# Moving the second layer's gate blocks, a longer warm-up and a last output in three token parts

## The chip, the cores and the metric

The kernel runs on one core of a Trainium2 chip. The metric is the device time of one execution in microseconds (us); less is better. The core's engines are TensorE (PE for its matmuls, PEld for its weight loads), VectorE (DVE), ScalarE (ACT), GpSimd (POOL, unused here) and SyncE (SP), whose queue issues nearly all DMAs.

## The reference, cut to what matters

The program is one inference step of a two-layer backbone on 640 tokens (512 latent tokens and 128 context tokens) of width 1024. Each layer is one mixer:

```
shift, scale, gate = split(silu(cond) @ ada_w[l] + ada_b[l], 3)
h = rms_norm(x) * (1 + scale) + shift
u = h @ w_in[l]
y = concat(A differential attention, B gated 3-tap convolution,
           C latent attention, D neighbourhood attention), each times silu(its gate path)
x = x + gate * (y @ w_out[l])
```

Latent and context tokens have different `cond`. After the second layer there is a final RMSNorm, `y = x * rsqrt(mean(x*x) + eps) * g`. Keys and values of the context tokens are returned too.

## The kernel before, in words

**Precision.** Every large matmul works on split operands: a float32 value is held as a high part and a low part (both in the fp32r type), and a product is three matmuls: high x high, high x low, low x high. Each matmul instruction loads its own 128x128 stationary operand (a weight load on PEld) and then streams the moving operand, whose columns are tokens or output features. Plain float32 matmuls, as those with `ones` or `cs`, show as two matmul records each in the trace.

**Order of work.** The program first builds a list of operations (`Plan.add`), and a planner (`Plan.schedule`) then puts them in one order for each engine, by ready times from a table of costs (`price`, `transfer`) and by a priority: the place in the list plus the group's number in the table `SHIFT`. Each engine then runs its own list strictly in that order. All operations are issued from L464. In the planner's costs an fp32r matmul of n columns is `0.4375 * n + 6` ns, and the next matmul may follow 58 ns after.

**Front.** `keep_warm(WARM[0])` puts matmuls of `ones` by `ones` ahead of everything, so that TensorE has work before the first data arrive. Then the first 384 tokens of x (eight DMAs) and the first layer's eight shift-and-scale blocks are loaded, each block as two halves of 512 KB (`adaw`). `ada_rows` multiplies a half by `cs` in eight narrow matmuls, and after each of the first four halves it adds further `keep_warm` matmuls (`WARM[1]` to `WARM[4]`), which have the lowest priority but must all be run. `at(h)` places other loads among the halves: the pieces of the first projection's weights after the halves named in `WA`, the other tokens after those in `X1`. `rms_rows` adds the squares of x, sums them over the partitions by a matmul with `ones`, and takes the inverse root; `finish` makes `hh` and `hl` of one 128-row slice of h once that slice's block is there.

**Gate blocks and the second layer's blocks.** The first layer's four gate blocks and all twelve blocks of the second layer come later, one at each call of `ada_next`: two 512 KB loads into the `wraw` buffers (three buffers, shared with the weight pieces), eight narrow matmuls, a copy, and two small stores to a DRAM buffer `adram`. `ada_end` reads the stored rows back, reduces them, transposes them twice and adds the biases into `modA`, `modB` (shift and scale) and `modG` (gate). In the first layer there are eleven calls in the fills `d`, `qk0`, `qk1` and `b`, and eight in the output projection; so the last five of the 16 blocks fall into that projection, and the second layer's first projection waits for the end of the last `ada_end` (`gate[0]`).

**Fills.** The projections whose results aren't needed at once (`z`, `d`, `qk0`, `qk1`, `b`) are placed among the twelve attention heads by `FILL`; their matmuls take up what the softmax chains leave free on TensorE.

**Output projection.** For each part of `HALVES[l]` and each of eight output blocks `fb`, 24 matmuls (eight slices, three products) of a 128x128 stationary weight by `c1 - c0` tokens fill one bank; VectorE multiplies by the gate and adds x; ScalarE squares. After a part, `rms_rows` sums the squares, and in the last layer the result is scaled in two halves and stored. Before, both layers have two parts: tokens 0 to 384 and 384 to 640.

Of the kernel before, what the change touches and what calls it, by code (L numbers as in the profile page):

```python
# [13 lines left out]
F32 = mybir.dt.float32  # L14
# [6 lines left out]

L = 2
X1 = (4, 4, 4, 4, 4, 4, 4, 4)
WA = (2, 6, 11, 16)
LATE = (16, 17)
HALVES = (((0, 384), (384, 640)), ((0, 384), (384, 640)))
START = ((0, 384), (384, 640))
RMS = ((0, 8), (0, 8))
YK = (0, 1, 4, 5, 2, 6, 3, 7)
# [3 lines left out]
SWAP = 1290  # L33
SILU = 8
SLOW, LATER = 1.1, 800
WARM = (15, 10, 8, 4, 4)
SHIFT = {"": 38, "a0": 47, "a1": -28, "ada0": -8588, "av0": 6296, "av1": 3, "b0": 25951, "b1": 24557, "c0": -2462, "d0": 62, "d1": 33941, "f0.0": -174, "f0.1": 22, "f1.0": -183, "f1.1": 2841, "h0.0": -4317, "h0.1": 205, "h1.0": 7, "h1.1": -10499, "h10.0": 1418, "h10.1": -8, "h11.0": 638, "h11.1": 4686, "h2.0": -3351, "h2.1": -22079, "h3.0": -2855, "h4.0": -2974, "h4.1": -2909, "h5.0": -1, "h5.1": -9, "h6.0": 797, "h6.1": -6113, "h7.0": 20, "h7.1": 13278, "h8.0": 5300, "h9.0": -7596, "lam": 6901, "o0.0": -505, "o1.0": -80, "o1.1": 26, "p0.0": 162, "p0.1": -20, "p2.0": -2125, "p2.1": 432, "p3.0": -1337, "p3.1": 4371, "p4.0": -1388, "p4.1": -27369, "p7.0": -1727, "p7.1": 960, "p8.1": -18800, "pa0": 51, "pa1": -552, "qk00": -18970, "qk01": 10605, "qk10": 10903, "qk11": 14623, "x0": -3000, "x1": 6892, "x2": -1536, "y0": -1625, "y1": 9425, "y2": -77, "z0": -13, "z1": -227}
FILL = (('z', 4), ('d', 6), ('qk0', 7), ('qk1', 8), ('b', 12))
D = 1024
NT = 640  # L40
# [11 lines left out]
BIAS_W = 1792  # L52
# [430 lines left out]
def body(ctx: ExitStack, tc: tile.TileContext, i, o):  # L483
# [12 lines left out]
    R = Plan()  # L496
# [52 lines left out]
                R.ops[-1].prio += 10 ** 6  # L549
                R.ops[-1].cost = {"PE": 215}  # L550
    keep_warm(WARM[0])
    for op in R.ops[-WARM[0]:]:
        op.cost = {"PE": 320}

    modA = R.tile([128, L, 8, 2], F32, name="modA")
    modB = R.tile([128, L, 8, 2], F32, name="modB")
# [13 lines left out]
    def wpiece(l, name, idx):  # L570
        if l == 0 and name == "a":
            at(WA[idx])
            R.offset += WBOOST
        else:
            R.offset = 0
        off, kk, n = PIECES[name][idx]
        src = i["win"][l, off:off + 128 * kk * n].rearrange("(p c) -> p c", p=128)
        return wsplit(src, kk, n)

    def wsplit(src, kk, n, place=None):  # L580
        raw = R.tile([128, 1024], F32, name="wraw", tag="wraw", bufs=3)
# [13 lines left out]
    def at(h):  # L595

        R.offset = ada_at[min(h, 15)] + 7.5 * max(h - 15, 0) + 0.5 - len(R.ops)

    def ada_rows(l, blk, raws, warm):
        pa = (ttile if warm else mmtile)()  # L600
        for hf, raw in enumerate(raws):
            for k in range(4):
                PE.matmul(pa[32 * k:32 * k + 32, 0:256], cs[:, 4 * hf + k, :], raw[:, 256 * k:256 * k + 256],
                          start=(hf == 0), stop=(hf == 1))
            if warm and 2 * blk + hf < 4:
                keep_warm(WARM[1 + 2 * blk + hf], len(R.ops) - 1)
        sb = R.tile([128, 256], F32, name="adasb", bufs=1)
        S.activation(sb, pa[:, 0:256], AF.Copy)
        return sb

    def ada_first(l, blk, places):

        for hf in range(2):
            ada_at.append(len(R.ops))
            SP.dma_start(places[hf], i["adaw"][l, blk, hf])
        sb = ada_rows(l, blk, places, True)
        pb = ttile()
        for c in range(2):
            PE.matmul(pb[:, 2 * c:2 * c + 2], sb[:, 128 * c:128 * c + 128], sel, start=True, stop=True)
        R.need = len(R.ops) - 1  # L620
        V.tensor_scalar(modB[:, l, blk], pb[:, 0:2], sp[:, l, blk:blk + 1], None, op0=OP.add)
        V.tensor_scalar(modA[:, l, blk], pb[:, 2:4], b1[:, l, blk:blk + 1],
                        sp[:, l, 24 + blk:25 + blk], op0=OP.add, op1=OP.mult)

    def ada_block(l, blk):

# [11 lines left out]
    def ada_end(l, b0, b1_):  # L638
        group, R.group = R.group, f"ada{gate[1]}"
        nb = b1_ - b0  # L640
        m = 2 * nb
        tag, n = ("wraw", 1024) if l == 0 else ("bias", BIAS_W)
        rows = R.tile([128, n], F32, name=tag, tag=tag, bufs=3 if l == 0 else 1)[0:m, 0:1024]
        SP.dma_start(rows, adram[l, b0:b1_].rearrange("b s k c -> (b s) (k c)"))
        su = R.tile([128, 256], F32, name="adasb", bufs=1)[0:m]
        V.tensor_reduce(su, rows.rearrange("p (k c) -> p c k", k=4), AX.X, OP.add)
        pt = mmtile()
        for c in range(2):
            PE.transpose(pt[:, m * c:m * c + m], su[:, 128 * c:128 * c + 128], ident[0:m, 0:m])
        v = pt[:, 0:2 * m].rearrange("p (c b s) -> p b c s", c=2, b=nb)  # L650
        wide = lambda t, n: t[:, :, None].to_broadcast([128, n, 2])
        if nb == 12:
            V.tensor_add(modB[:, l], v[:, 0:8, 0], wide(sp[:, l, 0:8], 8))
            V.tensor_add(modA[:, l], v[:, 0:8, 1], wide(b1[:, l], 8))
            V.tensor_mul(modA[:, l], modA[:, l], wide(sp[:, l, 24:32], 8))
        for c in range(2):
            V.tensor_add(modG[:, l, c:8:2], v[:, nb - 4:nb, c], wide(sp[:, l, 16 + c:24:2], 4))
        R.group = group

    later = [(0, b) for b in range(8, 12)] + [(1, b) for b in range(12)]  # L660

    def ada_next(l):

        if l == 0 and later:
            ll, blk = later.pop(0)
            ada_block(ll, blk)
            if blk == 11:
                ada_end(ll, 8 if ll == 0 else 0, 12)
                gate[0] = len(R.ops) - 1

    def rms_rows(xv, cuts=(0, 8), wide=False):
        w = xv.shape[2]
# [163 lines left out]
    for l in range(L):  # L836
        if l == 0:
# [28 lines left out]
            for n, x in enumerate(x_cur):  # L866
                R.group = f"x{n}"
                first = len(R.ops)
                rstds.append(rms_rows(x, RMS[n], n == 0))
                for op in R.ops[first:]:  # L870
                    op.deps.add(table)
            for kt in range(8):
                for n, (x, c, rstd) in enumerate(zip(x_cur, START, rstds)):
                    R.group = f"{'xy'[n]}{min(kt, 2)}"
                    finish(0, x, kt, *c, rstd)
# [321 lines left out]
        def fill_d():  # L1197
            SP.dma_start(dvt[:, 5], i["cdv"][l])

            def ev_d(t, acc):  # L1200
                evac_copy(dvt[:, t], acc)
            R.need = dst.ops[0]
            ada_next(l)
            tm_seq(l, "dv", ev_d)
            R.need = None
            SP.dma_start(o["sdv"][l], dvt[:, 4])

        def fill_qk(p):
            if p:
                hl = R.tile([128, 2, 1408], F32R, name="hl")  # L1210
            else:
                hl = dst[:, 1536:].rearrange("p (a n) -> p a n", a=2)
            raw = R.tile([128, 128], F32, name="cd", bufs=2)
            SP.dma_start(raw, i["cdk"][l, p])
            R.ops[-1].deps.add(R.begun)
            split(hl[:, 0, NT + 256:NT + 384], hl[:, 1, NT + 256:NT + 384], raw, lambda t: t.bitcast(F32))
            R.need = len(R.ops) - 1
            wh, wl = wpiece(l, f"dq{p}", 0)

            def ev_q(hf, c, acc):  # L1220
                hi, lo = hl[:, 0, c], hl[:, 1, c]
                S.activation(hi, acc, AF.Copy, scale=0.125)
                V.scalar_tensor_tensor(lo, acc, 0.125, hi.bitcast(F32), op0=OP.mult, op1=OP.subtract)
            ada_next(l)
            fm_mm(wh, wl, ev_q)
            wh, wl = wpiece(l, f"dk{p}", 0)

            def ev_k(hf, c, acc):
                k = slice(NT + 384 * hf, NT + 256 + 512 * hf)
                split(hl[:, 0, k], hl[:, 1, k], acc, lambda t: t.bitcast(F32))  # L1230
                if hf:
                    st = R.tile([128, 128], F32, name="cd", bufs=2)
                    evac_copy(st, acc[:, 256:384])
                    SP.dma_start(o["sdk"][l, p], st)
            ada_next(l)
            fm_mm(wh, wl, ev_k, 256)
            R.need = None
            ready["qk", p] = hl
# [85 lines left out]
                    R.tile([128, 1024], F32R, name="wk", tag="ks", bufs=2)) for n in range(2)]  # L1324
        big2 = R.tile([128, 4, 1024], F32R, name="wyt", tag="yt")
        places += [(big2[:, 2 * n], big2[:, 2 * n + 1]) for n in range(2)]
        c0, c1 = HALVES[l][1]
        xall = R.tile([128, 2816], F32, name="xall", tag="hl")[:, :8 * (c1 - c0)].rearrange("p (k c) -> p k c", k=8)
        SP.dma_start(xall, xsrc[:, :, c0:c1].rearrange("k p c -> p k c"))
        for hf, (c0, c1) in enumerate(HALVES[l]):  # L1330
            R.group = f"o{hf}.{l}"
            xn = xns[hf]
            for fb in range(8):
# [3 lines left out]
                wh, wl = wo[fb]  # L1337
                w = c1 - c0
                if hf:
                    xo = xall[:, fb]  # L1340
                else:
                    xo = R.tile([128, NT], F32, name="xo", tag=("osb", "q3")[fb % 2], bufs=(2, 4)[fb % 2])
                    SP.dma_start(xo[:, :w], xsrc[fb, :, c0:c1])
# [11 lines left out]
                if l + 1 < L:  # L1355
                    SP.dma_start(xdram[fb, :, c0:c1], xn[:, fb])
            R.group = f"f{hf}.{l}"
            rstd = rms_rows(xn, (0, 7, 8) if l + 1 == L and hf == 1 else (0, 8))
            if l + 1 < L:
                for kt in range(8):  # L1360
                    finish(l + 1, xn, kt, c0, c1, rstd)
# [123 lines left out]
```

## Time and profile before

| what | us |
|---|---|
| time, median of 3 runs (825.54 to 825.94) | 825.73 |
| the profiled execution's own time | 825.87 |
| span of its trace, first to last instruction | 824.1 |
| TensorE busy with matmuls in the span | 799.7 |
| VectorE busy | 578.9 |
| ScalarE busy | 505.0 |

A view of the trace gives, for an instruction or a merged run of them, the start and the length in us from the span's start, the engine, the operation, what is written and read ("out<-in", with the shape as partitions x elements), and in brackets how long the engine sat idle before it and what it waited for. Matmuls are pipelined: the length of one is its latency, and what a matmul costs in a stream is the distance from one start to the next. In the view of stages the busy times stand in the order PE, PEld, DVE, ACT, POOL, each with its count of instructions, and then TensorE's granted clock as a share of 2.4 GHz, the DMA engines' busy share and GB/s.

### The profile page before, as it was taken

To read this page: it belongs to the slowest core of one execution; us is meant where nothing else is said; L and a number is where in the kernel's file an instruction comes from. 1 tells how busy PE (TensorE), PEld (TensorE's weight loads), DVE (VectorE), ACT (ScalarE), POOL (GpSimd) and SP (SyncE) were. 2 spreads that over 40 slices of the span, in tenths; PEclk is the share of its full clock that TensorE was granted. 3 is DMA by queue.
4 is the path that set the end of the run, shared out by engine and by line. 5 is a ranking of instruction groups with operands and counts; after the bars stand their busy time and mean duration, and the time that the engine had idled before them with its cause. 6 is when DMAs were issued, how large, how long until landed. Compare 5 with 4: busy or idle time off the path is not lost.

```text
span 824.1 us, 14974 instructions
## 1 busy us (share of the span) xinstructions
PE 799.7 (97%) x5570; PEld 746.0 (91%) x5570; DVE 578.9 (70%) x1296; ACT 505.0 (61%) x1108; POOL 0.2 (0%) x4
## 2 busy tenths in 40 slices
PE   7999999998999999999999999999999999999995
PEld 6789898998898888989998899999999989999995
DVE  3744499798674985837367636986987899876643
ACT  5852487677883874624237436866887878645432
POOL 0000000000000000000000000000000000000000
PEclk8999999999999999999999999999999999999998
DMA  9924533444562787756650355333146646823221
GB/s 313 364 100 109 169 88 83 114 133 119 173 162 83 186 259 203 254 170 215 238 193 30 89 139 165 105 79 104 61 108 159 145 106 184 254 70 90 84 77 52
DMA packets 50029, 120.15 MB, mean 146 GB/s; under 512 B 7940, under 2 KB 21892, under 8 KB 49956
## 3 DMA queue, kind: packets, MB, share of 16 engines
q1 hardware_dynamic: 49812, 119.11, 48.2%
q8 instruction: 44, 0.72, 0.4%
q14 instruction: 29, 0.24, 0.1%
q10 hardware_dynamic: 144, 0.07, 0.0%
HBM read 82.69 MB, written 6.59 MB: 108 GB/s over the span
## 4 chain that ended last, share of the span: by engine, by line
PE 85%; ACT 5%; DVE 4%; DMA 3%; issue 1%; SPq 1%; DVEq 0%; ACTq 0%
PE bank L464 81%; PE pair L464 5%; ACT t L464 2%; ACT thi L464 1%; DVE t L464 1%; DMA wraw<-adaw 1%; DMA bias<-bias 1%; DVE tlo L464 1%; DMA yt<-adaw 1%; SPq L464 1%; DVE mn L464 1%; DMA q<-hl 0%; DVE cst L464 0%; ACT avt L464 0%; DVE adasb L464 0%
## 5 line engine op out<-in xcount | busy, mean ns | idle before, releaser
L464 PE MATMUL bank<-hh,whi 128*128 128x320 f32 (+2 forms) x640 | 202.2, 317 | 0.3 <-ACT adasb L464 0.3
L464 PE MATMUL bank<-hh,wlo 128*128 128x320 f32 (+2 forms) x640 | 201.0, 315 | 0.0
L464 PE MATMUL bank<-hl,whi 128*128 128x320 f32 (+2 forms) x640 | 200.7, 314 | 0.0
L464 PEld LDWEIGHTS bank<-hh,whi 128*128 128x128 f32 x640 | 120.5, 188 | 2.8 <-issue 1.2
L464 PEld LDWEIGHTS bank<-hh,wlo 128*128 128x128 f32 x640 | 120.3, 188 | 2.4 <-issue 1.6
L464 PEld LDWEIGHTS bank<-hl,whi 128*128 128x128 f32 x640 | 120.6, 188 | 2.1 <-issue 1.2
L464 DVE TENSOR_TENSOR wlo<-wraw,whi 128x1024 fp32r<-128x1024 f32 (+1 forms) x64 | 76.5, 1195 | 62.8 <-ACT whi L464 62.5
L464 ACT ACTIVATE thi<-bank 128x512 fp32r<-128x512 f32 (+3 forms) x164 | 76.8, 486 | 49.1 <-PE bank L464 45.4
L464 PE MATMUL bank<-whi,hl 128*128 128x256 f32 (+2 forms) x320 | 105.9, 332 | 0.0
L464 PE MATMUL bank<-whi,hh 128*128 128x256 f32 (+2 forms) x320 | 105.1, 333 | 0.7 <-DVE adst L464 0.5
L464 PE MATMUL bank<-wlo,hh 128*128 128x256 f32 (+2 forms) x320 | 105.1, 329 | 0.0
L464 DVE TENSOR_TENSOR tlo<-bank,thi 128x512 fp32r<-128x512 f32 (+3 forms) x164 | 86.8, 548 | 16.9 <-ACT thi L464 16.1
L464 ACT ACTIVATE whi<-wraw 128x1024 fp32r<-128x1024 f32 (+1 forms) x64 | 66.3, 1035 | 51.9 <-PE bank L464 40.6
L464 DVE TENSOR_REDUCE mn<-pair 128x1 f32<-128x640 f32 x96 | 77.9, 816 | 7.0 <-PE pair L464 4.4
L464 ACT ACTIVATE t<-pair,mn 128x640 f32<-128x640 f32 x96 | 75.9, 792 | 9.2 <-DVE mn L464 6.1
L464 PE MATMUL bank<-par,t 128*128 128x128 f32 x456 | 79.6, 274 | 1.4 <-DVE tlo L464 1.4
L464 PE MATMUL pair<-ks,qs 96*128 96x320 f32 (+1 forms) x256 | 62.9, 327 | 4.6 <-ACT t L464 4.3
L464 PEld LDWEIGHTS bank<-whi,hh 128*128 128x128 f32 x320 | 60.1, 189 | 6.6 <-issue 0.8
L464 PE MATMUL bank<-thi,vs 128*128 128x256 f32 (+3 forms) x224 | 64.3, 295 | 0.8 <-ACT t L464 0.8
L464 PEld LDWEIGHTS bank<-whi,hl 128*128 128x128 f32 x320 | 60.3, 188 | 5.1 <-issue 1.6
L464 PEld LDWEIGHTS bank<-wlo,hh 128*128 128x128 f32 x320 | 60.4, 189 | 5.0 <-issue 1.2
L464 PE MATMUL bank<-tlo,vs 128*128 128x256 f32 (+3 forms) x224 | 64.0, 303 | 0.5 <-DVE tlo L464 0.5
(191 smaller groups left out, 1450.7 us busy)
## 6 DMA issues: line engine op xcount, KB each, us to landing
wraw<-win SPq DMA_DIRECT2D x52, 512.0 KB, 4.1
wraw<-adaw SPq DMA_DIRECT2D x32, 512.0 KB, 4.8
ks<-hl SPq DMA_DIRECT2D x48, 192.0 KB, 3.6
wraw<-wout SPq DMA_DIRECT2D x16, 512.0 KB, 3.9
bias<-bias SPq DMA_DIRECT2D x8, 896.0 KB, 6.8
ks<-hl SPq DMA_DIRECT2D x48, 96.0 KB, 2.2
qs<-hl SPq DMA_DIRECT2D x48, 80.0 KB, 2.1
qs<-hl SPq DMA_DIRECT2D x24, 160.0 KB, 2.5
```

Of the source, the lines that this page charges most:

```text
L464: done = getattr(engines[op.engine], method)(*[fix(x) for x in args], **{k: fix(x) for k, x in kw.items()})
```

## The change

- `HALVES[1]`: the second layer's output projection runs in three token parts, 0 to 384, 384 to 512 and 512 to 640, where it had two. The x rows of the last two parts are still loaded at once (`xall`).
- `later` is split by layer. The first layer's calls of `ada_next` now work off twelve blocks (its own four gate blocks and the second layer's eight shift-and-scale blocks); the second layer's four gate blocks come in the second layer's fill `b`, with an `ada_end` of their own. `ada_end` therefore runs three times, where it ran twice.
- `WARM` puts 34 matmuls ahead of the first data, where it had 15, and 4, 4, 4, 4 after the first four halves, where it had 10, 8, 4, 4.
- `WA` moves the four pieces of the first projection's weights one or two halves forward.
- Two dependencies are added in the front: the sum over x's first part is multiplied before the second half of block 0 (`second`), and the first weight piece is split only after that part's inverse root (`R.rooted`). The two operations that end a block (`modB`, `modA`) get a higher priority.
- `SHIFT` is a new table, so that the planner's order of all groups is another.

```diff
-WA = (2, 6, 11, 16)
+WA = (0, 5, 10, 15)
-HALVES = (((0, 384), (384, 640)), ((0, 384), (384, 640)))
+HALVES = (((0, 384), (384, 640)), ((0, 384), (384, 512), (512, 640)))
-WARM = (15, 10, 8, 4, 4)
+WARM = (34, 4, 4, 4, 4)
-SHIFT = {"": 38, "a0": 47, "a1": -28, "ada0": -8588, ...
+SHIFT = {"": 38, "a0": 44, "a1": 69, "ada0": -10519, "ada1": 1159, ...
...
     keep_warm(WARM[0])
-    for op in R.ops[-WARM[0]:]:
-        op.cost = {"PE": 320}
+    for n, op in enumerate(R.ops[-WARM[0]:]):
+        op.cost = {"PE": 340 if n < 14 else 215}
...
-        return wsplit(src, kk, n)
+        split_at = len(R.ops) + 1
+        w = wsplit(src, kk, n)
+        if l == 0 and name == "a" and idx == 0:
+            R.ops[split_at].deps.add(R.rooted)
+        return w
...
+            if warm and blk == 0:
+                second.append(len(R.ops))
...
+        for op in R.ops[-2:]:
+            op.prio -= 3000
...
-        tag, n = ("wraw", 1024) if l == 0 else ("bias", BIAS_W)
+        tag, n = ("wraw", 1024) if nb == 4 else ("bias", BIAS_W)
...
-        if nb == 12:
+        if nb == 8:
...
-        for c in range(2):
-            V.tensor_add(modG[:, l, c:8:2], v[:, nb - 4:nb, c], wide(sp[:, l, 16 + c:24:2], 4))
+        for c in range(2 if nb == 4 else 0):
+            V.tensor_add(modG[:, l, c:8:2], v[:, :, c], wide(sp[:, l, 16 + c:24:2], 4))
...
-    later = [(0, b) for b in range(8, 12)] + [(1, b) for b in range(12)]
+    later = ([(0, b) for b in range(8, 12)] + [(1, b) for b in range(8)], [(1, b) for b in range(8, 12)])
...
-        if l == 0 and later:
-            ll, blk = later.pop(0)
+        if later[l]:
+            ll, blk = later[l].pop(0)
+            gate[1] = l
             ada_block(ll, blk)
-            if blk == 11:
-                ada_end(ll, 8 if ll == 0 else 0, 12)
-                gate[0] = len(R.ops) - 1
+            if blk in (7, 11):
+                ada_end(ll, 0 if blk == 7 else 8, blk + 1)
+                if l == 0:
+                    gate[0] = len(R.ops) - 1
...
+                if n == 0:
+                    R.rooted = len(R.ops) - 1
                 for op in R.ops[first:]:
                     op.deps.add(table)
+                    if n == 0 and "PE" in op.calls:
+                        for k in range(4):
+                            R.ops[second[1] + k].deps.add(op.n)
...
-            ada_next(l)
+            if l == 0:
+                ada_next(l)
...
-        c0, c1 = HALVES[l][1]
+        c0, c1 = HALVES[l][1][0], NT
...
-                    xo = xall[:, fb]
+                    xo = xall[:, fb, c0 - HALVES[l][1][0]:c1 - HALVES[l][1][0]]
...
-            rstd = rms_rows(xn, (0, 7, 8) if l + 1 == L and hf == 1 else (0, 8))
+            rstd = rms_rows(xn, (0, 7, 8) if l + 1 == L and hf == 2 else (0, 8))
```

The guard `if l == 0` stands at the calls of `ada_next` in the fills `d`, `qk0` and `qk1`; those in `b` and in the output projection have none.

## Rows read from the trace of the kernel before

**Rows 1.** The page: busy time by engine.
```profile
PE 799.7 (97%) x5570; PEld 746.0 (91%) x5570; DVE 578.9 (70%) x1296; ACT 505.0 (61%) x1108; POOL 0.2 (0%) x4
```
**Rows 2.** Stages: stretch, its length, busy time by engine, granted clock, DMA.
```profile
10.70:14.00 3.30, 3.29 (x20) 2.19 (x24) 0.14 (x1) 0.00 (x0) 0.00 (x0) 0.50 1.03 420
...
62.00:320.00 258.00, 249.57 (x1798) 232.39 (x1797) 193.87 (x440) 175.46 (x400) 0.00 (x0) 1.00 0.50 141
320.00:427.00 107.00, 107.00 (x773) 98.14 (x772) 60.09 (x124) 43.66 (x85) 0.00 (x0) 1.00 0.69 224
427.00:680.00 253.00, 250.69 (x1716) 239.31 (x1716) 196.72 (x433) 174.07 (x388) 0.00 (x0) 1.00 0.39 107
680.00:814.00 134.00, 134.00 (x921) 132.12 (x920) 91.53 (x212) 70.98 (x150) 0.00 (x0) 1.00 0.39 117
```
**Rows 3.** Timeline of PE: first matmul of the last part, and what follows its last.
```profile
790.54 0.28 PE L464 MATMUL bank<-hh,whi 128*128 128x256 f32 x1
...
813.97 0.59 PE L464 MATMUL bank<-thi,ones 128*128 128x256 f32 x2
```
**Rows 4.** Timeline of PE and PEld: short runs of fp32r matmuls of 128 columns.
```profile
340.86 0.28 PE L464 MATMUL bank<-thi,vs 128*128 128x128 f32 x1
340.92 0.19 PEld L464 LDWEIGHTS bank<-tlo,vs 128*128 128x128 f32 x1
340.98 0.27 PE L464 MATMUL bank<-tlo,vs 128*128 128x128 f32 x1
341.03 0.19 PEld L464 LDWEIGHTS bank<-hh,wlo 128*128 128x128 f32 x1
341.09 0.36 PE L464 MATMUL bank<-hh,wlo 128*128 128x320 f32 x1
```
**Rows 5.** Timeline of PE: the same matmuls right behind one of 320 columns.
```profile
271.37 0.31 PE L464 MATMUL bank<-hh,wlo 128*128 128x320 f32 x1
271.51 0.33 PE L464 MATMUL bank<-ks,qs 128*128 128x128 f32 x2
271.68 0.28 PE L464 MATMUL bank<-k,q 128*128 128x128 f32 x1
271.79 0.36 PE L464 MATMUL bank<-hh,whi 128*128 128x320 f32 x1
```
**Rows 6.** Timeline behind the last projection matmul.
```profile
814.17 0.61 DVE L464 SCALAR_TENSOR_TENSOR cst<-bank,modG,hl 128x128 f32<-128x128 f32 x2 [1.29 <-PE bank L464]
...
815.28 0.70 PE L464 MATMUL bank<-tlo,ones 128*128 128x256 f32 x2 [0.72 <-ACT tlo L464]
816.02 0.47 ACT L464 ACTIVATE thi<-bank,epst 128x256 f32<-128x256 f32 x1 [0.25 <-PE bank L464]
...
816.97 2.36 DVE L464 TENSOR_TENSOR cst<-cst,thi 128x1024 f32<-128x1024 f32 x2 [2.19 <-ACT thi L464]
818.23 1.55 SPq L464 DMA_DIRECT2D yt<-cst  x2
```
**Rows 7.** Timeline of the front.
```profile
1.05 5.93 PE L464 MATMUL bank<-ones 128*128 128x128 f32 x30 [1.05 <-DVE ones L464]
...
10.71 1.08 PE L464 MATMUL bank<-yt,cs 128*32 128x256 f32 x8 [3.74 <-DMA yt<-adaw]
...
11.72 2.08 PE L464 MATMUL bank<-ones 128*128 128x128 f32 x8
...
18.97 1.36 PE L464 MATMUL bank<-ones 128*128 128x128 f32 x10
...
20.83 0.96 PE L464 MATMUL bank<-whi,hh 128*128 128x512 f32 x3
```
**Rows 8.** Groups of PE by form, from 8 to 31 us: the warm-up matmuls.
```profile
L464 PE MATMUL bank<-ones 128*128 128x128 f32 x46 | 7.7, 318 | 0.0
```
**Rows 9.** Waits of PE, from 280 to 330 us and from 425 to 450 us.
```profile
PE bank L464 <- DMA wraw<-adaw: 0.9, 1, 0.9
...
PE bank L464 <- DVE adasb L464: 0.5, 1, 0.5
```

More of the change, by code (lines that the diff above doesn't have):

```diff
@@ L35 @@
 SLOW, LATER = 1.1, 800
-WARM = (15, 10, 8, 4, 4)
-SHIFT = {"": 38, "a0": 47, "a1": -28, "ada0": -8588, "av0": 6296, "av1": 3, "b0": 25951, "b1": 24557, "c0": -2462, "d0": 62, "d1": 33941, "f0.0": -174, "f0.1": 22, "f1.0": -183, "f1.1": 2841, "h0.0": -4317, "h0.1": 205, "h1.0": 7, "h1.1": -10499, "h10.0": 1418, "h10.1": -8, "h11.0": 638, "h11.1": 4686, "h2.0": -3351, "h2.1": -22079, "h3.0": -2855, "h4.0": -2974, "h4.1": -2909, "h5.0": -1, "h5.1": -9, "h6.0": 797, "h6.1": -6113, "h7.0": 20, "h7.1": 13278, "h8.0": 5300, "h9.0": -7596, "lam": 6901, "o0.0": -505, "o1.0": -80, "o1.1": 26, "p0.0": 162, "p0.1": -20, "p2.0": -2125, "p2.1": 432, "p3.0": -1337, "p3.1": 4371, "p4.0": -1388, "p4.1": -27369, "p7.0": -1727, "p7.1": 960, "p8.1": -18800, "pa0": 51, "pa1": -552, "qk00": -18970, "qk01": 10605, "qk10": 10903, "qk11": 14623, "x0": -3000, "x1": 6892, "x2": -1536, "y0": -1625, "y1": 9425, "y2": -77, "z0": -13, "z1": -227}
+WARM = (34, 4, 4, 4, 4)
+SHIFT = {"": 38, "a0": 44, "a1": 69, "ada0": -10519, "ada1": 1159, "av0": 16007, "av1": 9, "b0": 20030, "b1": 26350, "c0": -2945, "c1": 42, "d0": -15, "d1": 38724, "f0.0": -2291, "f0.1": 28, "f1.0": -149, "f1.1": -6505, "f2.1": 5395, "h0.0": -10485, "h0.1": 156, "h1.0": 530, "h1.1": -10253, "h10.0": -8183, "h10.1": 5207, "h11.0": 1303, "h11.1": -4230, "h2.0": -7939, "h2.1": -11378, "h3.0": -4585, "h3.1": -5938, "h4.0": -1665, "h4.1": -3836, "h5.0": 361, "h5.1": 5772, "h6.0": -3668, "h6.1": -5092, "h7.0": -1594, "h7.1": 11755, "h8.0": 8691, "h8.1": -2253, "h9.0": -8898, "h9.1": 127, "lam": 9366, "o0.0": -433, "o0.1": -17292, "o1.0": 19, "o1.1": 37, "o2.1": 133, "p0.0": -4226, "p0.1": -2567, "p2.0": -4412, "p2.1": 431, "p3.0": 310, "p3.1": 4183, "p4.0": -365, "p4.1": 906, "p7.0": -1937, "p7.1": 8479, "p8.0": -7953, "p8.1": -163, "pa0": -333, "pa1": -9550, "qk00": -11029, "qk01": 7846, "qk10": 11602, "qk11": 14431, "x0": 2128, "x1": 639, "x2": -3103, "y0": -12028, "y2": -19596, "z0": -15, "z1": -227}
 FILL = (('z', 4), ('d', 6), ('qk0', 7), ('qk1', 8), ('b', 12))
@@ L597, in at @@
         R.offset = ada_at[min(h, 15)] + 7.5 * max(h - 15, 0) + 0.5 - len(R.ops)
+    second = []
     def ada_rows(l, blk, raws, warm):
@@ L641, in ada_end @@
         m = 2 * nb
-        tag, n = ("wraw", 1024) if l == 0 else ("bias", BIAS_W)
-        rows = R.tile([128, n], F32, name=tag, tag=tag, bufs=3 if l == 0 else 1)[0:m, 0:1024]
+        tag, n = ("wraw", 1024) if nb == 4 else ("bias", BIAS_W)
+        rows = R.tile([128, n], F32, name=tag, tag=tag, bufs=3 if nb == 4 else 1)[0:m, 0:1024]
         SP.dma_start(rows, adram[l, b0:b1_].rearrange("b s k c -> (b s) (k c)"))
@@ L1223, in ev_q @@
                 V.scalar_tensor_tensor(lo, acc, 0.125, hi.bitcast(F32), op0=OP.mult, op1=OP.subtract)
-            ada_next(l)
+            if l == 0:
+                ada_next(l)
             fm_mm(wh, wl, ev_q)
@@ L1234, in ev_k @@
                     SP.dma_start(o["sdk"][l, p], st)
-            ada_next(l)
+            if l == 0:
+                ada_next(l)
             fm_mm(wh, wl, ev_k, 256)
```

## The prediction

> **What bounds the kernel now.** I read the page first: TensorE is busy 799.7 us of 824.1, VectorE 578.9, ScalarE 505.0 [rows 1]. So the time is TensorE's own stream plus 24.4 us in which it stands still, and an edit counts if it changes that stream's length or one of those gaps. The view of stages says where the gaps are: 258.0 - 249.6 = 8.4 us between 62 and 320, none between 320 and 427, 2.3 between 427 and 680, none between 680 and 814 [rows 2]. That is 10.7 us in the middle, spread over many short waits. What is left lies at the ends: 3.74 us before the first block of weights [rows 7], and 10 us behind the last projection matmul [rows 3, 6].
>
> The busy share hides one more thing. A matmul's row gives its latency; its cost is the distance to the next start. I therefore read the timeline for starts, and for the shape that the change brings in: fp32r matmuls of 128 columns in a long stream. The kernel before has such matmuls only in runs of a few, among the attention heads of the context tokens.
>
> **The third part of the last output.** Before, the last part runs from 790.54 to 813.97 [rows 3]: 8 blocks of 24 matmuls are 192 of 256 columns, and the first part's sum of squares, one plain float32 matmul (0.6, an estimate from the 0.59 of the like pair at 813.97), runs among them; (23.4 - 0.6) / 192 = 0.119 us each. After, the same columns come as 2 x 192 = 384 matmuls of 128 columns, each again with its own weight load.
>
> What one of these costs has two bounds in the trace. Behind a matmul of 320 columns the first starts at 271.51, and the next, the second of the pair, 0.06 later (the pair is 0.33 long, one of them 0.27); then come 0.11 (271.68) and 0.11 (271.79) [rows 5]. In a run where the one before is also narrow the starts lie 0.12 and 0.11 apart (340.86, 340.98, 341.09), and the weight loads keep the same step (340.92, 341.03) [rows 4]. The reading: a wide matmul gives the next weight load time to finish under it, so that one narrow matmul gets through in its column time; a narrow one doesn't, and then the load, at 0.11, sets the pace. In the new parts every matmul stands behind a narrow one. I take 0.112, the nearest row being the run of narrow ones: 384 x 0.112 = 43.0 us against 192 x 0.119 = 22.8, so **+20.2**. Bounds: 0.058 gives 22.3 us (-0.5), 0.115 gives 44.2 (+21.4). Nothing hides this: TensorE has no gap between 680 and 814 [rows 2], and the planner's own cost (62 ns) is no row of the trace.
>
> Weighed against the skill: the Trainium skill, page "TensorE: Matmul & The Clock Gate", section "Weight-path perf modes", has a fast weight load for 128 weights of a type that isn't FP32, with no win for 4-byte types. Were fp32r loaded that way, the sum would be the one at 0.058; rows 4 speak against it.
>
> The new part has a sum of squares of its own: one more plain float32 matmul, two records, **+0.25** (0.12 each, from 1.36 us for ten [rows 7]). Its ScalarE and VectorE steps lie under 21 us of matmuls: below nothing and above nothing alike, unless VectorE, now a third idle there, were full.
>
> **The end.** Behind the last matmul stands a chain that works on 256 columns and will work on 128 [rows 6]: the two gate steps become one (0.61 to about 0.35, -0.26); three ScalarE steps of up to 0.47 lose at most half, I take 0.11 each (-0.33); the float32 pair goes from 0.70 to about 0.45 (-0.25); the two closing multiplies halve (2.36 to 1.2, -1.16); the last store carries half the bytes (0 to -0.7, I take -0.2). Together **-2.2**, between -1.6 and -2.9.
>
> **The front.** Before, 30 records of warm-up end at 6.98, TensorE idles 3.74 us, and the first block half, at 10.71, runs at a granted clock of 0.50 (1.2 GHz) [rows 2, 7]: the warm-up records are then 0.21 apart (2.08 for eight, one 0.58 long), later 0.12 [rows 7]. After: 68 records. The first 30 take until 6.98 as now, the other 38 take 38 x 0.12 = 4.6 at full clock and end near 11.5, or 38 x 0.21 = 8.0 and end near 15 at half clock. Busy without a break, the engine should keep the full clock, so 11.5: the first half starts some 0.8 late and is done in 0.6 in place of 1.1. What is late next is the rest of block 0, which now stands behind the sum over x.
>
> The possible gain: between 8 and 31 us the warm-up matmuls behind the halves take 7.7 us of TensorE's time [rows 8] and must be run in their place in the order, data or no data. After, they are 16 matmuls, 32 records, 3.8 us at 0.12. Half clock costs about 2 us of real work (four halves at 1.08 for 0.6 [rows 7]). The first projection starts at 20.83 [rows 7] and from then on its matmuls and the blocks' keep TensorE busy until 62, so an earlier start is kept. The ceiling is 3.9 + 2 - 0.8 = 5.1; the floor is a loss of 0.8, if the data, not TensorE, hold it up, because the weight pieces that `WA` moves forward push later halves back in SP's queue (512 KB each). I take **-3.5**, nearer to the ceiling, since TensorE ran without a gap there.
>
> **The gate blocks.** Four blocks (8 loads of 512 KB, 8 stores, 32 matmuls and their copies) leave the first layer's output projection, where TensorE has no gap, and come to the second layer's convolution, where it has next to none either: their matmuls cancel. The first layer's boundary waits 0.5 us for `ada_end`'s reduction [rows 9]; with fewer blocks that goes (**-0.5**). A third `ada_end` adds two transposes (about 0.3), a readback on SP and a reduction on VectorE: **+0.3**; its result is needed only in the output projection. The loads share three buffers with the weight pieces: such a load held TensorE up for 0.9 once in the first layer [rows 9], so 0 to +1; I take 0, DMA share being 0.39 in the new place and 0.69 in the old [rows 2].
>
> **The new order.** `SHIFT` changes the order of all groups. It can at best take away the 10.7 us of waits in the middle and may add as many. No row tells which; I take **0**, with 3 to either side.
>
> **Sum.** 20.2 + 0.25 - 2.2 - 3.5 - 0.5 + 0.3 = +14.55. On the profiled execution's 825.87 (span 824.1 and 1.8 around it) that is 840.4; the median, 825.73, is 0.14 lower, so **840.3**.
>
> **Rivals.**
> - *The loads are hidden after all* (6 in 100; the side of faster). Long streams let PEld run ahead, and each narrow matmul costs 0.058. The part then takes 22.3 us: 840.3 - 20.7 = 819.6. For it: the first narrow matmul behind a wide one. Against it: every later one. It decides if the spacing falls below about 0.074, where the narrow parts cost no more than the other gains return (0.112 - 14.5 / 384 = 0.074).
> - *Half hidden* (5 in 100): narrow matmuls alternate with waiting wide ones, or loads come in pairs, mean 0.085, 32.6 us, 829.9. The skill's page named above, section "Back-to-back issue gap", gives about 81 ns for a sustained stream of 128-column matmuls with their loads; by that rule the part takes 31.1 us and the sum is 828.4. No run of rows 4 is that fast.
> - *The longer warm-up does nothing* (16 in 100): data hold the front up, and it starts late instead: +0.8 for -3.5, 844.6, or with an order that costs some more, up to 847.
> - *The new order fills the middle* (5 in 100): half of the 10.7 us goes, 834.9.
> - The forecast as summed: 68 in 100, 837 to 843.
>
> **Chances and range.** Under 0.2% (1.7 us) a measurement of this kernel can't tell a change from none. Faster: the first rival, 0.06. Same: part of the second, 0.02. Slower: the rest, 0.92. The range 834 to 847 leaves out the two cases of hidden loads; it takes in both ends of the front, of the spacing (0.11 to 0.115, -0.8 to +1.2) and of the order.
>
> **What would show it.** In the trace after: the last part's 384 matmuls with starts and weight loads 0.11 apart, some 43 us from the end of the first part to the last sum of squares; about 8 us from there to the end; the granted clock at 1.00 from 10.7 on, and the first projection's start some 3 to 4 us before 20.83; as many gaps in the middle as before. The prediction is wrong if narrow starts lie under 0.08 apart, if the planner puts the narrow parts between wide ones, or if the middle's gaps move by more than 3 us.

## The result, and the profile after

The changed kernel takes 838.31 us (median of 4 runs, 838.17 to 841.85) against 825.63 for the kernel before in the same runs: ratio 1.0167, 95% interval 1.0138 to 1.0196. It is slower by 12.7 us; 840.3 was predicted, 834 to 847 the range. The profiled execution took 838.42, its span is 836.5.

The page's first part, busy time by engine:

```profile
PE 821.9 (98%) x5784; PEld 767.2 (92%) x5784; DVE 582.6 (70%) x1304; ACT 508.5 (61%) x1128; POOL 0.2 (0%) x4
```

TensorE is busy for 22.2 us more than in [rows 1], with 214 more matmuls: 192 from the third part, 38 from 19 more warm-up matmuls ahead, 20 fewer from the ten behind the halves, and four from a third sum of squares and a third `ada_end`. The stages, columns as in [rows 2]:

```profile
10.70:14.00 3.30, 3.30 (x29) 2.29 (x27) 0.25 (x1) 0.00 (x0) 0.00 (x0) 1.00 1.02 420
...
62.00:320.00 258.00, 252.63 (x1813) 234.99 (x1813) 190.15 (x432) 175.19 (x403) 0.00 (x0) 1.00 0.53 148
320.00:427.00 107.00, 106.99 (x750) 100.81 (x749) 73.12 (x156) 51.56 (x99) 0.00 (x0) 1.00 0.54 173
427.00:680.00 253.00, 251.67 (x1731) 239.20 (x1730) 191.14 (x424) 171.20 (x390) 0.00 (x0) 1.00 0.43 118
```

From 10.7 us on the granted clock is 1.00, where it was 0.50. TensorE's gaps between 62 and 680 are 5.4 + 1.3 = 6.7 us; they were 10.7. So two of the three places got better. The third is the end of TensorE's timeline, the first matmuls of the narrow parts and the last:

```profile
784.92 0.34 PE L464 MATMUL bank<-hh,yt 128*128 128x384 f32 x1
785.10 0.22 PE L464 MATMUL bank<-hh,whi 128*128 128x128 f32 x1
785.16 0.27 PE L464 MATMUL bank<-hl,whi 128*128 128x128 f32 x1
785.27 0.28 PE L464 MATMUL bank<-hh,wlo 128*128 128x128 f32 x1
785.38 0.28 PE L464 MATMUL bank<-hh,whi 128*128 128x128 f32 x1
785.49 0.28 PE L464 MATMUL bank<-hl,whi 128*128 128x128 f32 x1
...
828.68 0.27 PE L464 MATMUL bank<-hh,yt 128*128 128x128 f32 x1
828.79 0.43 PE L464 MATMUL bank<-thi,ones 128*128 128x128 f32 x2
```

Read the first column. The first narrow matmul, behind one of 384 columns, gives way after 0.06; from the second on they start 0.11 apart, to the end of the part. The two narrow parts and the sum between them run from 785.10 to 828.79, 43.7 us; the one part that they replace ran from 790.54 to 813.97, 23.4 us [rows 3]. The chain behind, which answers to [rows 6]:

```profile
829.00 0.35 DVE L464 SCALAR_TENSOR_TENSOR cst<-bank,modG,hl 128x128 f32<-128x128 f32 x1 [1.66 <-PE bank L464]
...
829.74 0.49 PE L464 MATMUL bank<-tlo,ones 128*128 128x128 f32 x2 [0.51 <-ACT tlo L464]
830.27 0.37 ACT L464 ACTIVATE thi<-bank,epst 128x128 f32<-128x128 f32 x1
...
831.01 1.29 DVE L464 TENSOR_TENSOR cst<-cst,thi 128x512 f32<-128x512 f32 x2 [1.66 <-ACT thi L464]
831.73 1.34 SPq L464 DMA_DIRECT2D yt<-cst  x2
```

And the front, TensorE alone, against [rows 7]:

```profile
1.04 10.79 PE L464 MATMUL bank<-ones 128*128 128x128 f32 x68 [1.04 <-DVE ones L464]
11.76 0.64 PE L464 MATMUL bank<-yt,cs 128*32 128x256 f32 x8
12.33 1.16 PE L464 MATMUL bank<-ones 128*128 128x128 f32 x8
...
17.62 1.38 PE L464 MATMUL bank<-ones 128*128 128x128 f32 x10
...
19.84 0.50 PE L464 MATMUL bank<-whi,hh 128*128 128x512 f32 x1
...
58.18 0.40 PE L464 MATMUL bank<-whi,hl 128*128 128x512 f32 x1
```

The last row is the last matmul of the first layer's first projection; before, it started at 61.65. Before, 26 warm-up records stood inside that projection, 18 of them in one run; after, four do:

```profile
23.01 2.17 PE L464 MATMUL bank<-ones 128*128 128x128 f32 x18
```

Cut at four points of TensorE's timeline, the two traces differ thus (us):

| stretch | before | after | difference |
|---|---|---|---|
| start to the last matmul of the first projection | 61.65 | 58.18 | -3.47 |
| from there to the first matmul of the last output | 695.37 | 693.38 | -1.99 |
| first part, 384 columns | 33.52 | 33.54 | 0.0 |
| remaining columns, to the last sum of squares | 23.43 | 43.69 | +20.26 |
| the end behind | 10.09 | 7.69 | -2.40 |
| span | 824.06 | 836.48 | +12.4 |

In the second row TensorE's idle time fell from 10.7 to 6.8 us. Without the idle time that stretch grew, from 684.6 to 686.6, so only half of what the gaps gave was won.

### The profile page after: what moved, and what is told of

It is laid out like the page before. It is cut to its first block, busy times and chain, and to the rows that moved or that the text cites. A ratio compares the mean times of both kernels' runs of the same rounds, so it can differ in the third digit from the quotient of the medians.

```text
span 836.5 us, 15439 instructions
## 1 busy us (share of the span) xinstructions
PE 821.9 (98%) x5784; PEld 767.2 (92%) x5784; DVE 582.6 (70%) x1304; ACT 508.5 (61%) x1128; POOL 0.2 (0%) x4
## 4 chain that ended last, share of the span: by engine, by line
PE 91%; DMA 3%; DVE 2%; ACT 2%; SPq 1%; issue 1%; DVEq 0%; ACTq 0%
PE bank L464 85%; PE pair L464 6%; DMA wraw<-adaw 1%; ACT t L464 1%; SPq L464 1%; DMA ks<-adst 1%; DMA wraw<-wuq 0%; DVE tlo L464 0%; ACT thi L464 0%; DMA wraw<-win 0%; DVE wlo L464 0%; ACT whi L464 0%; DVE mn L464 0%; DVE adasb L464 0%; DVE t L464 0%
## 5 line engine op out<-in xcount | busy, mean ns | idle before, releaser
L464 PE MATMUL bank<-hh,whi 128*128 128x320 f32 (+3 forms) x656 | 205.9, 315 | 0.6 <-ACT yt L464 0.5
L464 PE MATMUL bank<-hl,whi 128*128 128x320 f32 (+3 forms) x656 | 206.2, 315 | 0.0
L464 PE MATMUL bank<-hh,wlo 128*128 128x320 f32 (+3 forms) x656 | 205.1, 314 | 0.0
L464 PEld LDWEIGHTS bank<-hh,whi 128*128 128x128 f32 x656 | 123.6, 189 | 3.4 <-issue 1.2
L464 PEld LDWEIGHTS bank<-hl,whi 128*128 128x128 f32 x656 | 123.8, 189 | 2.5 <-issue 1.6
L464 PEld LDWEIGHTS bank<-hh,wlo 128*128 128x128 f32 x656 | 123.5, 189 | 2.3 <-issue 1.2
```

The lines of the kernel that those rows point to most:

```text
L464: done = getattr(engines[op.engine], method)(*[fix(x) for x in args], **{k: fix(x) for k, x in kw.items()})
```

## The experiments

The prediction's theory: the narrow matmuls each cost a weight load, and that is the whole loss. Its rival: the parts are neutral and the loss sits in the gate blocks or the new order.

**Two parts again.** In the changed kernel:

```diff
-HALVES = (((0, 384), (384, 640)), ((0, 384), (384, 512), (512, 640)))
+HALVES = (((0, 384), (384, 640)), ((0, 384), (384, 640)))
...
-            rstd = rms_rows(xn, (0, 7, 8) if l + 1 == L and hf == 2 else (0, 8))
+            rstd = rms_rows(xn, (0, 7, 8) if l + 1 == L and hf == 1 else (0, 8))
```

> The changed kernel with the second layer's output projection back in two token parts; all else as changed, and the order of every engine up to that projection is the same. Theory (the narrow parts cost their weight loads, +20.3 us, +0.25 for a third sum, and give back 2.4 at the end): 838.3 - 18.1 = 820.2 us, the last part 22.8 us of matmuls again, about 10 us behind it. Rival (the loss sits elsewhere, in the gate blocks or the new order, and the parts are neutral): 836 to 839.

Measured: 820.43 us (4 runs), ratio to the kernel before 0.9938, interval 0.9919 to 0.9957. The loss was the third part, and without it the rest of the change is a gain. This version beats both kernels. Its last part starts 0.12 apart again:

```profile
786.42 0.28 PE L464 MATMUL bank<-hh,whi 128*128 128x256 f32 x1
786.53 0.28 PE L464 MATMUL bank<-hl,whi 128*128 128x256 f32 x1
786.65 0.28 PE L464 MATMUL bank<-hh,wlo 128*128 128x256 f32 x1
```

> The two-part kernel a second time, on the same chip as the kernel with the front's changes alone. 820.4 us; ratio to the kernel before 0.994.

Measured: 819.07, ratio 0.9937, interval 0.9922 to 0.9951.

**The third part alone.** The kernel before with only `HALVES[1]`, `xall` and the last `rms_rows` of the change.

> The kernel before with nothing but the third token part; the order of every engine up to that projection is that of before. Theory: 825.6 + 18.1 = 843.7 us. Rival (parts neutral, loss elsewhere): 824 to 827.

Measured: 846.16, ratio 1.0246, interval 1.0227 to 1.0264; +20.8 us where 18.1 was expected. The 384 narrow matmuls start 0.113 apart on the mean, as expected. Behind them this kernel is slower than the changed one: from the last narrow matmul to the end it takes 11.7 us, where the changed kernel takes 7.8. The rows of ScalarE and TensorE there:

```profile
832.55 0.44 PE L464 MATMUL bank<-thi,ones 128*128 128x128 f32 x2
...
833.03 0.37 ACT L464 ACTIVATE thi<-bank,epst 128x128 f32<-128x128 f32 x1 [12.54 <-PE bank L464]
...
836.76 0.79 PE L464 MATMUL bank<-thi,ones 128*128 128x128 f32 x2 [3.77 <-DVE thi L464]
```

The first row is the second part's sum of squares: in this kernel TensorE does it behind all of the third part's matmuls. ScalarE's fixed order puts the second part's inverse root ahead of the third part's squares; it waits 12.5 us for that sum, the squares are then done late, and TensorE waits 3.8 us for them. In the changed kernel ScalarE has the same order (the root at 810.17, the third part's first squares at 810.79), but TensorE does the second part's sum at 809.70, early among the third part's matmuls; the new table has numbers for these groups (`f1.1`, `f2.1`). So the third part also needed its entries in the table; the slow narrow matmuls are there with them and without.

**Wide and narrow by turns.** In the last layer the first and second token part run together:

```diff
+                both = [(hf, c0, c1, xo)]
+                if hf == 0 and l + 1 == L:
+                    both.append((1, *HALVES[l][1], xall[:, fb, 0:HALVES[l][1][1] - HALVES[l][1][0]]))
+                accs = [mmtile() for _ in both]
                 for n, kt in enumerate(YK):
-                    PE.matmul(acc[:, :w], wh[:, kt], hh[kt][:, c0:c1], start=(n == 0), stop=False)
...
+                    for m, (a, b) in enumerate(((wh, hh), (wh, hl), (wl, hh))):
+                        for acc, (_, e0, e1, _) in zip(accs, both):
+                            PE.matmul(acc[:, :e1 - e0], a[:, kt], b[kt][:, e0:e1], start=(n == 0 and m == 0),
+                                      stop=(n == 7 and m == 2))
```

> The changed kernel, with the first and second token part of the last output run together: each matmul of 384 columns is followed by one of 128 columns with the same weights, for all 192 pairs; the third part comes after, as changed. The prediction's reading (a narrow matmul behind a wide one gets through in 0.058, its load hidden under the wide one): a pair takes 0.174 + 0.058, 192 x 0.232 = 44.6 us in place of 33.5 + 21.8 = 55.3, time 827.6 us. Rival (a narrow matmul costs a load of 0.112 wherever it stands; behind a wide one half of it shows on the next start): a pair takes 0.286, 54.9 us, time 838 us.

Measured: 837.7 (one run). Each row is one wide and one narrow matmul:

```profile
752.02 0.45 PE L464 MATMUL bank<-hl,whi 128*128 128x384 f32 x2
752.31 0.46 PE L464 MATMUL bank<-hh,wlo 128*128 128x384 f32 x2
752.61 0.45 PE L464 MATMUL bank<-hh,whi 128*128 128x384 f32 x2
```

The pairs start 0.29 apart (mean of 192: 0.286), which is 0.174 + 0.112. So a narrow matmul costs 0.112 between wide ones too. The 0.06 from a narrow one's start to the next isn't a saving: the next wide one takes 0.227 in place of 0.174. The prediction had read [rows 5] otherwise, though the trace of before had it already, one row further on:

```profile
271.99 0.31 PE L464 MATMUL bank<-hl,whi 128*128 128x320 f32 x1
```

The 320-column matmul at 271.79, behind narrow ones, takes 0.20 to this start; behind another wide one it takes 0.147.

**Shorter loads.** Moving columns and count as changed, but 64 weight columns in 18 of 24 matmuls of the narrow parts:

```diff
+                    m = 64 if w == 128 and n not in (0, 7) else 128
-                    PE.matmul(acc[:, :w], wh[:, kt], hh[kt][:, c0:c1], start=(n == 0), stop=False)
+                    PE.matmul(acc[0:m, :w], wh[:, kt, 0:m], hh[kt][:, c0:c1], start=(n == 0), stop=False)
```

> The changed kernel, with weights of 64 columns in place of 128 in 18 of the 24 matmuls of each block of the two narrow parts (the first and the last slice keep 128, so that the bank is written whole); half of those products is left out. Moving columns and instructions are as changed. Theory (the weight load sets the pace): the 288 short-load matmuls fall from 0.112 to about 0.058, 16 x (6 x 0.112 + 18 x 0.058) = 27.5 us in place of 43.7, time about 822 us. Rival (a fixed floor for each matmul instruction of about 0.11, whatever it loads): no change, 838 us.

Measured: 822.41 (one run). Matmuls with 64 weight columns, and their loads:

```profile
786.03 0.22 PE L464 MATMUL bank<-hh,whi 128*64 128x128 f32 x1
786.09 0.22 PE L464 MATMUL bank<-hl,whi 128*64 128x128 f32 x1
786.15 0.22 PE L464 MATMUL bank<-hh,wlo 128*64 128x128 f32 x1
786.21 0.22 PE L464 MATMUL bank<-hh,whi 128*64 128x128 f32 x1
...
786.09 0.13 PEld L464 LDWEIGHTS bank<-hh,wlo 128*64 128x64 f32 x1
786.15 0.14 PEld L464 LDWEIGHTS bank<-hh,whi 128*64 128x64 f32 x1
```

They start 0.06 apart, with the same moving columns, and the loads keep that step. So no floor for each instruction sets 0.11; it goes with the weight columns, as a load's time would. The rows of the result halve with the weight columns, so this run can't tell the load from the writing of the result. What sets 0.06 stays open as well.

**The front, in two steps**, both on the two-part kernel and put in when instructions are issued, so that every engine's planned order stays. Of the 34 first warm-up matmuls only 15:

```diff
     keep_warm(WARM[0])
+    R.skip.update(op.n for op in R.ops[-WARM[0] + 15:])
...
         for op in self.schedule():
+            if op.n in self.skip:
+                continue
```

> The two-part kernel of the first experiment (820.4 us), of whose 34 first warm-up matmuls only 15 are issued; every engine's order is otherwise the same, since they are left out after planning. The full-clock theory: TensorE idles about 3.7 us again before the first half, runs at half clock until about 16 us, and the first layer's first projection, which ends at 58.3 there, ends 1 to 2 us later; time 821.4 to 822.4. Rival (the front's gain is that fewer warm-up matmuls stand behind the halves, or that the loads come in another order): end at 58.3, time 820.4.

Measured: 820.39, ratio 0.9939, interval 0.9917 to 0.9962. The trace shows the step, the time doesn't:

```profile
1.04 5.71 PE L467 MATMUL bank<-ones 128*128 128x128 f32 x30 [1.04 <-DVE ones L467]
10.89 1.08 PE L467 MATMUL bank<-yt,cs 128*32 128x256 f32 x8 [4.14 <-DMA yt<-adaw]
...
59.53 0.40 PE L467 MATMUL bank<-whi,hl 128*128 128x512 f32 x1
```

TensorE idles 4.1 us, and the first half takes 1.08 in place of 0.64. From the first half's start to the first projection it takes 10.3 us, where the two-part kernel takes 8.1 (11.33 to 19.41): the half clock costs 2.2 us. At the projection's last matmul, 59.53 in place of 58.30, 1.2 of them are left, because the first half starts 0.4 earlier here and the two-part kernel's projection takes 0.5 longer, most of it waits. In the profiled runs the later front then met its loads without waiting: the two-part kernel stood 3.2 us for `adaw` loads between 62 and 700, this one not at all. Whether it is always so, one profile each can't tell; 1.2 us of 820 lie within the interval.

Ten more warm-up matmuls behind the first two halves:

```diff
                 keep_warm(WARM[1 + 2 * blk + hf], len(R.ops) - 1)
+                R.again[len(R.ops) - 1] = (6, 4, 0, 0)[2 * blk + hf]
```

> The two-part kernel with ten more warm-up matmuls behind the first two halves (six and four, as many as the kernel before has there), put in after planning, every order else the same. If warm-up matmuls in TensorE's order cost their time: 10 x 0.24 = 2.4 us, the first projection ends near 60.7, time 822.8. Rival (they stand where TensorE would wait for data or for the other engines anyway): no change, 58.3 and 820.4.

Measured: 821.2, ratio 0.9946, interval 0.9928 to 0.9964; the last matmul of the first projection starts at 59.08, 0.8 later. That 0.8 isn't the price of the ten matmuls:

```profile
1.04 9.40 PE L465 MATMUL bank<-ones 128*128 128x128 f32 x68 [1.04 <-DVE ones L465]
10.38 0.64 PE L465 MATMUL bank<-yt,cs 128*32 128x256 f32 x8
...
20.69 0.50 PE L465 MATMUL bank<-whi,hh 128*128 128x512 f32 x1
```

From the first half to the first projection it takes 10.3 us in place of 8.1, with no gap: the ten matmuls cost 2.2 us there, which is 20 records at the 0.112 that lies between two of the 68 at full pace. But the same 68 warm-up records took 9.40 us in this execution, and 10.36 in the two-part kernel's, so the first half started 0.95 earlier; and the 0.5 us of the two-part kernel's projection are absent here too. In all the profiles with 34 matmuls ahead, the records are 0.21 apart at first and later about 0.11. The step comes between 4.4 and 7.2 us, in each execution at another time, and the first half starts between 10.38 and 11.76.

**Gate blocks back, old order, both.** On the two-part kernel: one list of 16 blocks in the first layer, with `ada_end` and the calls of `ada_next` as before; the old table `SHIFT`; and both, which is the kernel before with the front's changes alone.

```diff
-    later = ([(0, b) for b in range(8, 12)] + [(1, b) for b in range(8)], [(1, b) for b in range(8, 12)])
+    later = [(0, b) for b in range(8, 12)] + [(1, b) for b in range(12)]
```

> The two-part kernel with the second layer's gate blocks back in the first layer (one list of 16 blocks, two calls of ada_end), replanned. The prediction's step (matmuls cancel, boundary 0.5 to be had, third ada_end 0.3): 820.4 + 0.2, with the order's noise 819.5 to 821.5. Rival (the two microseconds that the middle gained come from this move): 822.4, with the wait for ada_end's reduction at the layer's boundary again.

Measured: 825.83, ratio 1.0012, interval 0.9996 to 1.0028.

> The two-part kernel with the old table SHIFT, all else as changed, replanned. If the new order is worth what the middle gained (2 us between the end of the first projection and the start of the last output) or more: 822.4 or above, with more idle time of TensorE between 62 and 680 us. Rival (the order is worth nothing; the middle's gain is the gate blocks or chance): 820.4.

Measured: 826.75, ratio 1.0018, interval 1.0007 to 1.003.

> The kernel before with the front's changes alone (warm-up, weight pieces, the two dependencies, the priorities of modA and modB): two parts, gate blocks in the first layer, old table. Together with the two-part kernel (820.4: new gates, new table), old gates with the new table (825.8) and new gates with the old table (826.8) it makes a square of four. If gate move and table each bring their gain by themselves, the corners add: 825.8 + 826.8 - 820.4 = 832.2 us. Rival (each table is fitted to its own placement, so a mixed pair is what costs, and the front's 3.5 us are the gain): about 822, the first projection ending near 58.

Measured: 822.52, ratio 0.9972, interval 0.9959 to 0.9985; the first projection's last matmul starts at 58.39. The corners don't add (832.2 would be the sum): each table is fitted to its own placement, and by the ratios a mixed pair costs about 3 to 4 us against the front alone. TensorE's waits of the gates-back kernel between 425 and 760 us show part of it:

```profile
PE bank L464 <- ACT hh L464: 2.2, 1, 2.2
PE bank L464 <- DVE tlo L464: 2.0, 4, 1.1
...
PE bank L464 <- DVE adasb L464: 0.5, 1, 0.5
```

The 0.5 us for `ada_end`'s reduction is back, as in [rows 9]; the larger waits are elsewhere, at the layer's boundary and in the second layer's last heads. Behind the boundary's wait of 2.2 us for `hh` the granted clock fell to 0.50, from 443.45 to 446.86; with the old table it was 0.50 from 649.98 to 653.39, and in that profile the first projection also waited 2.0 us for an `adaw` load. No other profile has a fall of the clock between 62 and 800 us. Half pace for 3.4 us is up to 1.7 us of each loss, an estimate from that length. New gates and new table together take 822.52 to 819.07 on the same chip: 3.4 us.

## Why the prediction was right, point by point

- **The narrow parts, +20.2 and +0.25.** Measured +20.26 together. The step rested on the spacing of short runs of narrow matmuls [rows 4], and it held in a stream of 384. The kernels with two parts again and with the third part alone show that the loss is theirs, and the halved loads that the pace goes with the weight columns. The first rival (loads hidden) and the second (half hidden) fell. Of the two sentences that leaned on the Trainium skill, page "TensorE: Matmul & The Clock Gate", the rule of the section "Back-to-back issue gap" (about 81 ns for each 128-column matmul with its load) doesn't hold here; the trace has 0.112. The fast load of "Weight-path perf modes" isn't seen for fp32r.
- **The reading of why** was half wrong: a wide neighbour doesn't hide a narrow matmul's load. It changed no number, since the narrow ones stand among themselves.
- **The end, -2.2.** Measured -2.40: multiplies 2.36 to 1.29, gate steps 0.61 to 0.35, the float32 pair 0.70 to 0.49, as worked out.
- **The front, -3.5.** Measured -3.47 at the end of the first projection, in three pieces. The first half started 1.05 late (0.8 was said). From there to the first projection it took 8.08 in place of 10.11, -2.03, at full clock (2 was said, but from four halves at 1.08; only two ran so, at 10.71 and 13.73, and the rest were warm-up matmuls and the sum over x). The projection took 38.34 in place of 40.82, -2.48, with no gap in either: TensorE runs the same there but for 22 warm-up records fewer, 2.5 at 0.112. So both gains named were there, but the fewer warm-up matmuls gave 2.5 and not 3.9; that price came from the busy time of 46 records, ten of them at half clock. The -3.5 was chosen between a floor and a ceiling, so that it fits so closely is in part luck, the more as the first half starts up to 1.4 us earlier in other executions. The sign given failed: the projection started 1.0 us earlier, not 3 to 4, because most of the saved matmuls had stood inside it. The order of loads and the two dependencies weren't tried by themselves; these pieces leave nothing for them here. In the time the front alone gives 2.1 us (822.52 against 824.58; the interval is 1.2 to 3.4).
- **Gate blocks -0.2 and new order 0.** Measured -1.99 in this profile, and 3.4 us in the medians of the pair on one chip. This is the term that was too small, and the prediction's own sign says so: the middle's gaps went from 10.7 to 6.7, by 4.0, and a move of more than 3 was to show it wrong. Between 62 and 700 us the longest waits of the heads, those for ScalarE's `t`, fell from 4.3 to 1.7, and those for `tlo` from 1.9 to 0.6. The rival that fills half of the gaps, given 5 in 100, was nearer to that than the forecast. Gate blocks and order were costed one by one, and they work only together. The term makes 1.8 of the 2.0 us by which the prediction was above the result. One pair of profiles wouldn't bear it: with the order of before, the profile of the third part alone took 693.85 in the middle, 1.5 less than 695.37. The medians do.

## What to carry to other kernels

Before a tile is cut narrower along the moving side, look up what one matmul with its weight load costs at that width in a stream: in this kernel 256 columns and 128 cost nearly the same, 0.119 and 0.112, so cutting a 256-column part in two buys 2.4 us at the end for 20 in the middle. Take the cost from distances between starts over a whole run of neighbours, since one row can show a debt that the next one pays. Before a difference in one profile is put down to an edit, compare the pieces between two points of the same work: in the front the start moved by up to 1.4 us with the moment at which full pace began. And where an order is fitted as a whole, a move of work and the order must be tried together and apart; here neither showed its worth alone.

## What the runs showed of the hardware that was not expected

- An fp32r matmul of 128 moving columns costs 0.112 us with 128 weight columns and 0.06 with 64, in a stream of its like.
- Between wide ones it costs the same 0.112: the pair with 384 columns takes 0.286, though its own start-to-start distance shows only 0.06.
- With 19 of 34 warm-up matmuls left out, TensorE idle for 4.1 us and the first work at half its speed (1.08 for 0.64 us), the time didn't move clear of the noise (ratios to the kernel before 0.9939 and 0.9938).
- The same 68 warm-up records ahead of the data took from 9.40 to 10.79 us, as the step from 0.21 to about 0.11 between starts came at another time in each execution.
